# A 64-byte against a 192-byte offset for one half of the stationary weights' split buffers, in a two-block transformer kernel on one core

## The chip, the cores and the metric

The kernel runs on one core of one Trainium2 chip. The metric is the device time of one execution in microseconds: the median of three runs. Lower is better.

## The reference, cut to what matters

Two transformer blocks run one after the other over 256 tokens of width 1024, in float32. They hold six feed-forward stages, an mLSTM and gating mixer, a pooling and SSD mixer, and an attention mixer. Most of the work is products of the tokens with large weights:

```
def swiglu(x, w_in, w_out):
    gate, up = jnp.split(x @ w_in, 2, axis=-1)
    return (jax.nn.silu(gate) * up) @ w_out

x = x + 0.5 * swiglu(rmsnorm(x, ffn1_norm_g[l]), ffn1_w_in[l], ffn1_w_out[l])
proj = xn @ w_mix_in[l]
```

## The kernel before, in words

**Splitting.** Each float32 factor `a` is written as a rounded part `hi` (type fp32r) and a remainder `lo = a - hi`, and a product is three matmuls, `ah*bh + ah*bl + al*bh` (`mm3`, lines 508 to 512). The normalised and transposed tokens stand in `xh` and `xl`, each `[128, 8, 256]`: eight slices of 128 channels with 256 tokens.

**Weights.** They come from memory in units. SyncE's queue loads raw tiles (`_load_raw`), and `_split_one` (line 337) splits one unit: ScalarE writes `hi` (line 357), VectorE writes `lo` (line 358). The two halves stand in one buffer `t` of shape `[128, 2, DP]`, with `DP = D + 64 = 1088` elements of 4 bytes: 1024 are used, 64 are spare. There are six such buffers in the pool `split` (tile name `sp`), and up to eight slots that stages lend while they don't need them (tile name `sx`).

**Two ways to use a unit.** In token mode (`in_chunk`, `out_pass`, `out_half_pass`) the tokens are stationary and the weights stream past, 512 columns a matmul, in the attention stage also 384 and 288. In channel mode the weights are stationary and the tokens stream, 256 columns a matmul. A channel-mode unit is a `cols` unit whose sixth field is 8 (`_mtile`): 128 output channels, with all eight slices of 128 by 128 side by side. `chan_chunk` (in `ffn`, from its third chunk on, output tile `tp`) and `m_tile` (in `mix` and `ssd`, output tile `mm`) take such a unit and make 24 matmuls of it, for each slice `k` one on line 510 (`hi`, streaming `xh`), one on line 511 (`hi`, streaming `xl`) and one on line 512 (`lo`, streaming `xh`). Every matmul has a weight load of its own (PEld in the profile), which TensorE runs while the matmul before it still streams.

```
o = SHIFT if self.units[u][0] == "cols" and self.units[u][5] == 8 else 0
hi, lo = t[:, 0, o:o + D], t[:, 1, o:o + D]
```

**Where the bytes stand.** For a channel-mode unit both parts begin `SHIFT = 16` elements, 64 bytes, into their half; for all other units at 0. The pools put every split buffer, every slot, and `xh` and `xl` 192 bytes past a multiple of 512 bytes in each partition (from the allocated addresses: the first split buffer at 40640, `xh` at 161472, `xl` at 169664). A half is 4352 bytes, 256 past a multiple of 512. So, counted modulo 512, a slice of `hi` of a channel-mode unit begins at 192 + 64 = 256, a slice of `lo` at 192 + 256 + 64 = 0, and the tokens that stream past begin at 192.

**Order.** The program's order on each engine is fixed when it is built (`tick`, `pump`, `after`): splits run ahead of use as buffers come free.

Of the kernel before, what the change touches and what calls it, by code (L numbers as in the profile page):

```python
# [14 lines left out]
D = 1024  # L15
# [7 lines left out]
NEG = -1.0e30  # L23


DP = D + 64
SHIFT = 16

# [88 lines left out]
def _size(u):  # L119
    return D if u[0] == "rows" else u[5] * sum(b - a for a, b in u[3])  # L120
# [112 lines left out]
class Builder:  # L233
# [103 lines left out]
    def _split_one(self):  # L337
        u = self.next_split
        gi, base, last = self.group_of[u]
        while self.next_raw <= gi:  # L340
            self._load_raw()
        n = _size(self.units[u])
        src = self.raws[gi][:, base:base + n]
        if self.main_free:
            self.main_free -= 1
            self.where[u] = None
            t = self.p_split.tile([P, 2, DP], F32R, tag="sp", name="sp")
        else:
            w = self.extra_free.pop(0)
            self.where[u] = w  # L350
            t = self.slot(w, [P, 2, DP], F32R, "sx") if w < 8 else None
        if t is None:
            hi, lo = (self.p_gate.tile([P, D], F32R, tag="gate", name="sg") for _ in range(2))
        else:
            o = SHIFT if self.units[u][0] == "cols" and self.units[u][5] == 8 else 0
            hi, lo = t[:, 0, o:o + D], t[:, 1, o:o + D]
        self.nc.scalar.activation(out=hi[:, 0:n], in_=src, func=AF.Copy)  # L357
        self.nc.vector.tensor_tensor(out=lo[:, 0:n], in0=src, in1=hi[:, 0:n], op=ALU.subtract)  # L358
        self.ready[u] = (hi, lo)
        self.next_split += 1  # L360
        if last:
            del self.raws[gi]
            while self.next_raw < len(self.offs) and len(self.raws) < self.RAW_BUFS:
                self._load_raw()
# [1505 lines left out]
```

## Time and profile before

| | |
|---|---|
| median of 3 runs | 1651.04 us (1649.2 to 1651.7) |
| the profiled execution's own time | 1650.13 us |
| its span, first to last instruction | 1648.3 us |
| around the span | 1.8 us |
| granted TensorE clock, mean | 0.996 of full speed |
| TensorE matmul (PE) busy | 1612.2 us, 98% |
| TensorE weight load (PEld) busy | 1446.2 us, 88% |
| VectorE / ScalarE / GpSimd busy | 1180.0 / 821.1 / 53.2 us |
| moved from memory | 361 MB, 220 GB/s over the span |

Matmuls overlap in the pipeline, so the busy time of one matmul (276 to 281 ns in channel mode) is not what it costs. What it costs is its *step*: the time from its start to the start of the next one. The timeline view shows starts, and a step is read from a long stretch as the last start less the first, over the number of matmuls between.

### The profile page before, as it was taken

Reading aid. Unit: us, or ns where it says so; the run is one execution under the profiler, and the core shown is the slowest. Engines: PE = TensorE matmul, PEld = TensorE weight load, DVE = VectorE, ACT = ScalarE, POOL = GpSimd, SP = SyncE. Lnnn points to the kernel's source line nnn. Section 1 sums busy time; section 2 is a strip of 40 time slices with the busy share of each in tenths; the row PEclk is TensorE's granted clock in tenths of the full one; section 3 lists DMA queues with packets and bytes.
Section 4 is the critical chain, followed back from the end, with each engine's and each line's share of the span. In section 5 each row is a group of like instructions: output and inputs, shape, how many; then the busy total and the mean of one; then the engine's idle time right before and its main releaser. Section 6 shows DMA issues by size and latency. Waiting matters only on the chain.

```text
span 1648.3 us, 25287 instructions
## 1 busy us (share of the span) xinstructions
PE 1612.2 (98%) x10290; PEld 1446.2 (88%) x10290; DVE 1180.0 (72%) x1729; ACT 821.1 (50%) x1161; POOL 53.2 (3%) x81
## 2 busy tenths in 40 slices
PE   8999999999999999999999999999999999999997
PEld 6999889888799988999898789998999987879996
DVE  6699578796688866877687777766777576676653
ACT  6544465445554446444465464445444366555442
POOL 0000001100000000000004000000000010000000
PEclk9999999999999999999999999999999999999999
DMA  8789344666488845888244269873788343147640
GB/s 296 278 320 329 143 178 154 233 252 225 189 308 292 288 161 206 319 302 297 101 156 152 102 252 340 296 287 119 285 299 296 140 170 151 52 179 256 226 170 26
DMA packets 62469, 363.80 MB, mean 221 GB/s; under 512 B 7056, under 2 KB 7184, under 8 KB 28944
## 3 DMA queue, kind: packets, MB, share of 16 engines
q1 hardware_dynamic: 62208, 362.10, 60.8%
q8 instruction: 81, 1.33, 0.3%
q14 instruction: 36, 0.29, 0.1%
q10 hardware_dynamic: 144, 0.08, 0.0%
HBM read 361.11 MB, written 1.05 MB: 220 GB/s over the span
## 4 chain that ended last, share of the span: by engine, by line
PE 90%; DVE 4%; ACT 4%; issue 1%; DMA 1%; POOL 0%; POOLq 0%; SPq 0%; ACTq 0%; DVEq 0%
PE tp L512 14%; PE tp L510 14%; PE tp L511 14%; PE mm L510 7%; PE mm L512 7%; PE mm L511 7%; PE mm L695 7%; PE mm L696 7%; PE mm L702 7%; DVE sp L358 1%; ACT sp L357 1%; PE tp L623 1%; DMA raw<-in_wts 1%; ACT xn L640 1%; ACT xn L591 1%
## 5 line engine op out<-in xcount | busy, mean ns | idle before, releaser
L358 DVE TENSOR_TENSOR sp<-raw,sp 128x1024 fp32r<-128x1024 f32 (+2 forms) x375 | 453.6, 1220 | 214.7 <-ACT sp L357 213.7
L357 ACT ACTIVATE sp<-raw 128x1024 fp32r<-128x1024 f32 (+2 forms) x375 | 390.0, 1050 | 378.9 <-PE tp L512 202.8
L510 PE MATMUL tp<-xh,sp 128*128 128x256 f32 x1032 | 289.7, 281 | 0.2 <-ACT gate L468 0.2
L512 PE MATMUL tp<-xh,sp 128*128 128x256 f32 x1032 | 289.1, 280 | 0.0
L511 PE MATMUL tp<-xl,sp 128*128 128x256 f32 x1032 | 289.1, 280 | 0.0
L358 DVE TENSOR_TENSOR sx<-raw,sx 128x1024 fp32r<-128x1024 f32 x161 | 196.2, 1221 | 92.3 <-ACT sx L357 92.0
L357 ACT ACTIVATE sx<-raw 128x1024 fp32r<-128x1024 f32 x161 | 169.4, 1055 | 172.5 <-PE tp L512 121.6
L511 PEld LDWEIGHTS tp<-xl,sp 128*128 128x128 f32 x1032 | 197.3, 191 | 0.9
L510 PE MATMUL tp<-xh,sx 128*128 128x256 f32 x696 | 195.8, 281 | 0.8 <-ACT gate L468 0.8
L512 PE MATMUL tp<-xh,sx 128*128 128x256 f32 x696 | 195.4, 281 | 0.0
L511 PE MATMUL tp<-xl,sx 128*128 128x256 f32 x696 | 195.4, 281 | 0.0
L510 PEld LDWEIGHTS tp<-xh,sp 128*128 128x128 f32 x1032 | 193.7, 188 | 1.4 <-ACT gate L468 0.5
L512 PEld LDWEIGHTS tp<-xh,sp 128*128 128x128 f32 x1032 | 193.8, 188 | 0.0
L432 DVE SCALAR_TENSOR_TENSOR mraw<-mraw,c_act 128x1024 f32<-128x1024 f32 x144 | 175.3, 1218 | 0.0
L510 PE MATMUL mm<-sp,xh 128*128 128x512 f32 (+2 forms) x340 | 133.0, 391 | 1.8 <-ACT xh L644 1.8
L511 PEld LDWEIGHTS tp<-xl,sx 128*128 128x128 f32 x696 | 133.3, 192 | 0.9
L510 PEld LDWEIGHTS tp<-xh,sx 128*128 128x128 f32 x696 | 130.6, 188 | 1.9 <-ACT gate L468 1.0
L512 PEld LDWEIGHTS tp<-xh,sx 128*128 128x128 f32 x696 | 130.7, 188 | 0.0
L512 PE MATMUL mm<-sp,xl 128*128 128x512 f32 (+2 forms) x340 | 130.0, 382 | 0.2
L511 PE MATMUL mm<-sp,xh 128*128 128x512 f32 (+2 forms) x340 | 129.4, 381 | 0.0
L695 PE MATMUL mm<-sp,hT 128*128 128x512 f32 x246 | 96.6, 393 | 1.8 <-ACT hT L869 1.4
L696 PE MATMUL mm<-sp,hT 128*128 128x512 f32 x246 | 96.2, 391 | 0.0
(472 smaller groups left out, 2793.3 us busy)
## 6 DMA issues: line engine op xcount, KB each, us to landing
raw<-in_wts SPq DMA_DIRECT2D x260, 1024.0 KB, 5.3
mraw<-in_mod SPq DMA_DIRECT2D x144, 512.0 KB, 5.5
raw<-in_wts SPq DMA_DIRECT2D x4, 768.0 KB, 4.6
raw<-in_wts SPq DMA_DIRECT2D x5, 512.0 KB, 5.2
row<-in_rows SPq DMA_DIRECT2D x3, 512.0 KB, 5.9
raw<-in_wts SPq DMA_DIRECT2D x2, 576.0 KB, 4.0
rows<-in_rows SPq DMA_DIRECT2D x2, 512.0 KB, 6.5
bp<-in_pool SPq DMA_DIRECT2D x1, 1024.0 KB, 7.6
```

What stands on the lines that cost most here:

```text
L357: self.nc.scalar.activation(out=hi[:, 0:n], in_=src, func=AF.Copy)
L358: self.nc.vector.tensor_tensor(out=lo[:, 0:n], in0=src, in1=hi[:, 0:n], op=ALU.subtract)
L432: nc.vector.scalar_tensor_tensor(out=src, in0=src, scalar=1.0, in1=self.c_act, op0=ALU.mult, op1=ALU.mult, accum_out=acc[:, kt:kt + 1])
L510: nc.tensor.matmul(out, ah, bh, start=first, stop=False)
L511: nc.tensor.matmul(out, ah, bl, start=False, stop=False)
L512: nc.tensor.matmul(out, al, bh, start=False, stop=last)
L591: nc.scalar.activation(out=xn[:, sl], in_=x[:, sl], func=AF.Square, scale=1.0 / 32.0, accum_out=ss[:, h:h + 1])
L623: nc.tensor.transpose(ps[:, j, :], src[:, k * P:(k + 1) * P], self.ident)
L640: nc.scalar.activation(out=vb[1][:, j], in_=banks[1][:, j], func=AF.Identity, scale=g[:, 4 + j:5 + j], bias=sh[:, 4 + j:5 + j])
L695: nc.tensor.matmul(accs[t][h], ah, hi[:, sl], start=(k == 0), stop=False)
L696: nc.tensor.matmul(accs[t][h], ah, lo[:, sl], start=False, stop=False)
L702: nc.tensor.matmul(accs[t][h], al, hi[:, sl], start=False, stop=False)
```

## The change

The offset becomes a pair: `hi` stays 16 elements (64 bytes) into its half, `lo` stands 48 elements (192 bytes) into its half. This holds for channel-mode units only.

```
-SHIFT = 16
+SHIFT = (16, 48)
...
-            o = SHIFT if self.units[u][0] == "cols" and self.units[u][5] == 8 else 0
-            hi, lo = t[:, 0, o:o + D], t[:, 1, o:o + D]
+            a, b = SHIFT if self.units[u][0] == "cols" and self.units[u][5] == 8 else (0, 0)
+            hi, lo = t[:, 0, a:a + D], t[:, 1, b:b + D]
```

No instruction is added, removed or moved: on all five engines the two programs have the same instructions in the same order with the same waits, and every tile has the same address. What differs is one address in 244 splits (the output of line 358, once for each channel-mode unit) and in 1952 matmuls and their loads (line 512 with a stationary `lo`, eight for each unit). Modulo 512, the `lo` slices move from 0 to 128; `hi` stays at 256, the streaming tokens at 192. The remainder then ends at element 48 + 1024 = 1072 of 1088.

## Rows read from the trace of the kernel before

**Rows 1.** The page: busy time by engine, and the chain that ended last.
```profile
PE 1612.2 (98%) x10290; PEld 1446.2 (88%) x10290; DVE 1180.0 (72%) x1729; ACT 821.1 (50%) x1161; POOL 53.2 (3%) x81
...
PE 90%; DVE 4%; ACT 4%; issue 1%; DMA 1%; POOL 0%; POOLq 0%; SPq 0%; ACTq 0%; DVEq 0%
```

**Rows 2.** Groups by line and form, PE: operands, count | busy us, mean ns | idle before.
```profile
L510 PE MATMUL tp<-xh,sp 128*128 128x256 f32 x1032 | 289.7, 281 | 0.2 <-ACT gate L468 0.2
...
L510 PE MATMUL tp<-xh,sx 128*128 128x256 f32 x696 | 195.8, 281 | 0.8 <-ACT gate L468 0.8
...
L510 PE MATMUL mm<-xh,sp 128*128 128x256 f32 x224 | 63.8, 285 | 0.0
```

**Rows 3.** Timeline of PE, a whole chunk (start, duration, instruction): one slow stretch.
```profile
59.63 0.28 PE L510 MATMUL tp<-xh,sp 128*128 128x256 f32 x1
...
70.94 0.40 PE L695 MATMUL mm<-sx,hT 128*128 128x512 f32 x1
```

**Rows 4.** Timeline of PE, three units of a later chunk: one fast stretch.
```profile
176.26 0.28 PE L510 MATMUL tp<-xh,sp 128*128 128x256 f32 x1
...
184.42 0.40 PE L695 MATMUL mm<-sp,hT 128*128 128x512 f32 x1
```

**Rows 5.** Groups of weight loads by form, stretch 59.8 to 70 us (slow).
```profile
L511 PEld LDWEIGHTS tp<-xl,sp 128*128 128x128 f32 x16 | 3.1, 192 | 0.0
L512 PEld LDWEIGHTS tp<-xh,sp 128*128 128x128 f32 x16 | 3.0, 188 | 0.0
L510 PEld LDWEIGHTS tp<-xh,sp 128*128 128x128 f32 x15 | 2.8, 188 | 0.0
```

**Rows 6.** The same, stretch 174 to 184 us (fast).
```profile
L512 PEld LDWEIGHTS tp<-xh,sp 128*128 128x128 f32 x23 | 4.3, 188 | 0.0
L511 PEld LDWEIGHTS tp<-xl,sp 128*128 128x128 f32 x23 | 4.3, 188 | 0.0
```

**Rows 7.** Groups of weight loads by form, whole span.
```profile
L511 PEld LDWEIGHTS tp<-xl,sp 128*128 128x128 f32 x1032 | 197.3, 191 | 0.9
L512 PEld LDWEIGHTS tp<-xh,sp 128*128 128x128 f32 x1032 | 193.8, 188 | 0.0
...
L511 PEld LDWEIGHTS tp<-xl,sx 128*128 128x128 f32 x696 | 133.3, 192 | 0.9
L512 PEld LDWEIGHTS tp<-xh,sx 128*128 128x128 f32 x696 | 130.7, 188 | 0.0
...
L511 PEld LDWEIGHTS mm<-xl,sp 128*128 128x128 f32 x224 | 42.2, 188 | 0.1
L512 PEld LDWEIGHTS mm<-xh,sp 128*128 128x128 f32 x224 | 42.1, 188 | 0.0
```

**Rows 8.** Timeline of PE, stationary weights of 8 columns (tile skw), 256 streamed.
```profile
214.88 0.28 PE L510 MATMUL tp<-xh,skw 128*8 128x256 f32 x1
...
216.75 0.28 PE L511 MATMUL tp<-xl,skw 128*8 128x256 f32 x1
216.86 0.28 PE L512 MATMUL tp<-xh,skw 128*8 128x256 f32 x1
...
217.54 0.28 PE L512 MATMUL tp<-xh,skw 128*8 128x256 f32 x1
```

**Rows 9.** Timeline of PE, token mode with 384 and with 288 streamed columns.
```profile
1338.05 0.33 PE L512 MATMUL mm<-sp,xl 128*128 128x384 f32 x1
...
1340.65 0.33 PE L512 MATMUL mm<-sp,xl 128*128 128x384 f32 x1
...
1346.35 0.29 PE L512 MATMUL mm<-sp,xl 128*128 128x288 f32 x1
...
1347.95 0.29 PE L512 MATMUL mm<-sp,xl 128*128 128x288 f32 x1
```

**Rows 10.** Groups by form: the splits on VectorE, and what VectorE waited for.
```profile
L358 DVE TENSOR_TENSOR sp<-raw,sp 128x1024 fp32r<-128x1024 f32 x364 | 444.0, 1230 | 205.9 <-ACT sp L357 204.9
...
L358 DVE TENSOR_TENSOR sx<-raw,sx 128x1024 fp32r<-128x1024 f32 x160 | 195.2, 1223 | 91.1 <-ACT sx L357 90.8
```

## The prediction

> **What bounds the kernel now.** Read the page first: TensorE's matmuls cover 98% of the span and 90% of the chain that ended last [rows 1]. Then the groups by form, for the matmuls whose weights the change touches: 1032 + 696 + 224 on line 510, and as many on lines 511 and 512, so 3 × 1952 = 5856 channel-mode matmuls. They hardly ever wait: 0.2, 0.8 and 0.0 us of idle time on line 510 [rows 2]. So what counts is the step from one start to the next, and a nanosecond on each step is 5.9 us of the kernel.
>
> Then the timeline, and there the steps fall into two paces. In the chunk from 59.63 to 70.94 us, 96 matmuls take 11.31 us: 117.8 ns a step [rows 3]. From 176.26 to 184.42 us, 72 matmuls of the same form take 8.16 us: 113.3 ns a step [rows 4]. Same operands' shapes, same clock, same addresses modulo 512; the streams fall into one pace or the other and then hold it for microseconds. I call them slow and fast; they are 4.5 ns apart.
>
> The weight loads show where the slow pace differs. In the slow stretch one load in three takes 192 ns, the others 188 [rows 5]; in the fast stretch all take 188 [rows 6]. This gives the count of slow steps. Over the span, the loads of line 511 are longer than those of line 512 by 197.3 - 193.8 = 3.5 us, 133.3 - 130.7 = 2.6 us and 0.1 us: 6.2 us in all [rows 7]. At 4 ns each that is 1550 slow trios of 1952, so 4650 slow steps and 1206 fast ones. It is an estimate: in `mix` and `ssd` the long load need not be on line 511, so slow steps may be missing.
>
> **The change part by part.**
>
> *Instructions.* None is added, removed or moved on any engine or queue, no wait is added, and no DMA changes. Nothing to price.
>
> *The write of the remainder.* VectorE's 244 outputs on line 358 land 128 bytes further on. The splits of the two buffer kinds, which mix shifted and unshifted outputs, take 1230 and 1223 ns [rows 10]; if the place cost or gave those 7 ns it would be 244 × 7 = 1.7 us of VectorE work, under the 205.9 + 91.1 us that VectorE idles ahead of these very instructions [rows 10]. The cover is that TensorE does not wait for splits [rows 2]; without it the 1.7 us would show. I take 0.
>
> *The read of the remainder.* This is the whole question: 1952 loads read from another place while `xl` streams, and nothing in the trace shows a stationary operand at 128 modulo 512 in channel mode. So the price is bounded from both sides by the nearest rows.
>
> - Gain, near end: only the stretch of the long load goes. That is 6.2 us if all of it was on the path [rows 7]. A second row agrees in size: with stationary weights of 8 columns, where hardly anything is loaded, 16 steps of the slower pace take 216.75 - 214.88 = 1.87 us, 116.9 ns a step [rows 8], 0.9 ns under 117.8; on 4650 steps that is 4.2 us.
> - Gain, in proportion: one load in three is moved, and the steps that it decides go at the fast pace: 1550 × 4.5 ns = 7.0 us [rows 3, 4].
> - Gain, far end: the slow pace can't keep itself up once one of its three loads is changed, and all slow steps become fast: 4650 × 4.5 ns = 20.9 us. That a slow stretch can fall into the fast pace and stay is seen in the 8-column weights: from 216.86 to 217.54 us, six steps take 0.68 us, 113.3 ns [rows 8].
> - Loss: token mode shows a still slower step. 15 steps of 384 columns take 2.60 us, 173.3 ns; 12 steps of 288 take 1.60 us, 133.3 ns [rows 9]. The line through them falls by 0.417 ns a column, and at 256 columns it gives 133.3 - 13.3 = 120.0 ns. If all channel-mode steps went to that, it would cost 4650 × 2.2 + 1206 × 6.7 = 10.2 + 8.1 = 18.3 us; if one in three did, 6.1 us.
>
> Between a gain of 20.9 and a loss of 18.3 us I take the gain in proportion, 7.0 us: it is next to the 6.2 us that the load rows carry directly [rows 7], and these are the only rows in which the loads differ between the two paces.
>
> The sum: 1650.1 us for the profiled execution, less 7.0, is 1643.1 us. The median of the runs shown, 1651.0, stands 0.9 us above the profiled execution, so for a median I say 1644.
>
> *A rule that speaks against it.* The rows show the pace of a stream and the length of its loads going together: 192 and 188 ns at 117.8 a step, 188 alone at 113.3 [rows 3 to 6]. The Trainium skill, page "SBUF — State Buffer", section "Who interferes with whom", gives TensorE two independent read ports, one for the streaming operand and one for weight loads, and says that it never waits on anyone. By that rule the place of the remainder changes nothing and the sum would be 1650.1 us. The trace agrees only in part: a port that nobody disturbs does not explain the 4 ns [rows 5, 6].
>
> **The rivals.**
>
> *No change: the place does not matter (1650 us).* The two paces are a matter of phase between loads and streams, not of addresses. For it: `hi` at 256 and `lo` at 0 modulo 512 already stand at different places, and it is a load of `hi` that is long while the load of `lo` is not [rows 5]; the weights of line 510 and line 511 are the very same bytes, and one is long, the other not. The 8-column weights begin at eight places 32 bytes apart, and the pace goes on for 16 steps all the same [rows 8]. Against it: 8-column loads read too little to meet anything for long, and the two places used now differ by 256 bytes, so they say nothing of a difference of 128. Time: 1650.1, between 1647 and 1653.
>
> *The fast stretches are lost (1655.5 us).* The fast pace needs all three steps of a trio at 113.3 ns. If the moved load makes its step just longer than that, no stretch can stay fast: 1206 steps fall back to 117.8, 1206 × 4.5 = 5.4 us more. It decides as soon as the step on line 512 alone exceeds 113.3 ns by any constant amount. For it: the fast pace is the rarer one, 1206 of 5856, and token mode, whose stationary tokens stand level with the streamed weights (192 modulo 512, streams from 192 or 448), never shows it: 133.3 and 173.3 lie on a line to 120.0 [rows 9]. Against it: the loads of `lo` have no long row now [rows 5, 7]. If the slow steps go to 120.0 as well, it is 18.3 us and 1668.4.
>
> *The whole slow pace goes (1629.2 us).* It is the far end of the forecast, not a case of its own: the same mechanism, 20.9 us.
>
> **How the numbers follow.** A difference of 0.2%, 3.3 us, is about what a measurement of this kernel can tell from no change. Forecast, the slow pace is weakened or broken: 0.47. Likeliest within it is 1644, its own range 1628 to 1647. No change: 0.33, because most of what the rows say of addresses is that they don't matter, but none of them tests a step of 128 bytes. Lost fast stretches, or steps towards 120.0: 0.20; there is a row for such a step, and nothing that ties it to this place. Low end: 1650.1 - 20.9 = 1629.2, with a margin 1628. High end: 1657, which takes in no change and the lost fast stretches (1655.5), and leaves out the steps towards 1668. What is left out is about 0.1 above and 0.05 below. So faster 0.47, same 0.33, slower 0.20.
>
> **What would show it.** The forecast is right if the chunk of rows 3 starts its 96 matmuls in clearly less than 11.31 us (11.17 for a third of the steps at the fast pace, 10.88 for all), if the loads of lines 511 and 512 come closer than 6.2 us in sum, and if the splits, the transfers and the token-mode steps stay as they are. It is wrong if the chunk takes 11.31 us again with one 192 ns load in three: then the place does not matter. The rival of lost fast stretches is right if the 72 matmuls of rows 4 take 8.48 us in place of 8.16. The prediction would also be wrong if VectorE's splits changed by more than the 7 ns between their two groups, since then something other than TensorE's reads would be at work.

## The result, and the profile after

| | before | after |
|---|---|---|
| median of 4 runs | 1651.13 us | 1630.45 us (1628.16 to 1632.76) |
| ratio, 95% interval | | 0.9877 [0.9858, 0.9896] |
| the profiled execution's own time / span | 1650.13 / 1648.3 us | 1632.14 / 1630.4 us |
| granted TensorE clock, mean | 0.996 | 0.996 |

The changed kernel is 20.7 us faster by the medians; the interval reaches from 17.2 to 23.4 us. The forecast was 7.0. The profiled execution of the changed kernel is one of its slower ones, so the two profiles are 18.0 us apart; the account below is of these two.

The page of the changed kernel, busy time by engine and the chain that ended last:

```profile
PE 1593.5 (98%) x10290; PEld 1427.6 (88%) x10290; DVE 1179.7 (72%) x1729; ACT 821.8 (50%) x1161; POOL 53.1 (3%) x81
...
PE 89%; DVE 5%; ACT 4%; DMA 1%; issue 1%; POOL 0%; POOLq 0%; SPq 0%; ACTq 0%; DVEq 0%
```

Against [rows 1], the matmuls are busy for 18.7 us less and the loads for 18.6 us less; the other engines differ by less than 1 us. TensorE still sets the time. Now the groups by form of the channel-mode matmuls, lines 511 to 513 (the change adds one line, so `mm3` stands one line further down):

```profile
L511 PE MATMUL tp<-xh,sp 128*128 128x256 f32 x1032 | 285.7, 277 | 0.2 <-ACT gate L469 0.2
...
L511 PE MATMUL tp<-xh,sx 128*128 128x256 f32 x696 | 192.8, 277 | 0.8 <-ACT gate L469 0.8
```

These are the groups of [rows 2], 4.0 and 3.0 us shorter, and each of the three lines has lost about as much. The timeline says how. First the chunk of [rows 3], entered from a token-mode matmul of 512 columns (line 703):

```profile
59.31 0.61 PE L703 MATMUL mm<-sp,hT 128*128 128x512 f32 x2
59.76 0.28 PE L511 MATMUL tp<-xh,sp 128*128 128x256 f32 x1
59.88 0.28 PE L512 MATMUL tp<-xl,sp 128*128 128x256 f32 x1
...
60.47 0.28 PE L511 MATMUL tp<-xh,sp 128*128 128x256 f32 x1
...
60.92 0.28 PE L512 MATMUL tp<-xl,sp 128*128 128x256 f32 x1
...
70.67 0.40 PE L696 MATMUL mm<-sx,hT 128*128 128x512 f32 x1
```

The 96 matmuls take 70.67 - 59.76 = 10.91 us, 113.6 ns a step, where they took 11.31. The stretch starts at the slow pace: its first six steps take 0.71 us, 118 ns each. Then it settles by itself: from 60.92 on, 86 steps take 9.75 us, 113.4 ns. The stretch of [rows 4], which was fast before, comes again to 8.16 us over 72 steps:

```profile
173.59 0.28 PE L511 MATMUL tp<-xh,sp 128*128 128x256 f32 x1
...
181.75 0.40 PE L696 MATMUL mm<-sp,hT 128*128 128x512 f32 x1
```

The long loads are gone. Groups of weight loads by form, whole span, against [rows 7]:

```profile
L512 PEld LDWEIGHTS tp<-xl,sp 128*128 128x128 f32 x1032 | 193.8, 188 | 0.9
...
L513 PEld LDWEIGHTS tp<-xh,sp 128*128 128x128 f32 x1032 | 193.7, 188 | 0.0
...
L513 PEld LDWEIGHTS tp<-xh,sx 128*128 128x128 f32 x696 | 130.7, 188 | 0.0
L512 PEld LDWEIGHTS tp<-xl,sx 128*128 128x128 f32 x696 | 130.7, 188 | 0.9
```

**Unit by unit.** The 5856 channel-mode matmuls are 244 units of 24. I took the mean step of each unit from its 13th matmul on, when it has settled. Before, 46 units had under 115 ns and 198 had 117.8. After, all 244 have 113.3 to 113.6.

**The account of the two profiles.** 198 slow units × 24 × 4.5 ns = 21.4 us could go. Summed from the starts in the timeline, the channel-mode steps take 688.3 us before and 668.8 after: 19.5 us less. Of the 1.9 us that are missing, 1.6 lie in the first twelve steps of the units that do not follow another channel-mode unit; these steps stay slow, as in the chunk above. Token mode gives 1.9 us back: the median step of 512 columns is 227 ns in both, but 163 of the 3375 steps are longer than 250 ns, where 154 were, and their sum goes from 804.3 to 806.2 us. 19.5 - 1.9 = 17.6 of the 17.9 us by which the spans differ.

Splits and their slack, groups by form on VectorE:

```profile
L359 DVE TENSOR_TENSOR sp<-raw,sp 128x1024 fp32r<-128x1024 f32 x364 | 444.1, 1230 | 197.5 <-ACT sp L358 196.5
L359 DVE TENSOR_TENSOR sx<-raw,sx 128x1024 fp32r<-128x1024 f32 x160 | 195.2, 1222 | 82.8 <-ACT sx L358 82.4
```

Their durations are those of [rows 10]; VectorE idles 16.7 us less ahead of them: the same work now stands in a shorter kernel.

### The profile page after: what moved, and what is told of

Same layout as the page of the kernel before. It is cut to its first block, busy times and chain, and to the rows that moved or that the text cites. A ratio compares the mean times of both kernels' runs of the same rounds, so it can differ in the third digit from the quotient of the medians.

```text
span 1630.4 us, 25287 instructions
## 1 busy us (share of the span) xinstructions
PE 1593.5 (98%) x10290; PEld 1427.6 (88%) x10290; DVE 1179.7 (72%) x1729; ACT 821.8 (50%) x1161; POOL 53.1 (3%) x81
## 4 chain that ended last, share of the span: by engine, by line
PE 89%; DVE 5%; ACT 4%; DMA 1%; issue 1%; POOL 0%; POOLq 0%; SPq 0%; ACTq 0%; DVEq 0%
PE tp L513 13%; PE tp L511 13%; PE tp L512 13%; PE mm L511 7%; PE mm L513 7%; PE mm L512 7%; PE mm L696 7%; PE mm L697 7%; PE mm L703 7%; DVE sp L359 2%; DMA raw<-in_wts 1%; ACT sp L358 1%; ACT xn L641 1%; PE tp L624 1%; ACT xn L592 1%
## 5 line engine op out<-in xcount | busy, mean ns | idle before, releaser
L511 PE MATMUL tp<-xh,sp 128*128 128x256 f32 x1032 | 285.7, 277 | 0.2 <-ACT gate L469 0.2
L513 PE MATMUL tp<-xh,sp 128*128 128x256 f32 x1032 | 285.1, 276 | 0.0
L512 PE MATMUL tp<-xl,sp 128*128 128x256 f32 x1032 | 285.0, 276 | 0.0
L358 ACT ACTIVATE sx<-raw 128x1024 fp32r<-128x1024 f32 x161 | 169.7, 1057 | 165.1 <-PE tp L513 113.6
L512 PEld LDWEIGHTS tp<-xl,sp 128*128 128x128 f32 x1032 | 193.8, 188 | 0.9
L511 PE MATMUL tp<-xh,sx 128*128 128x256 f32 x696 | 192.8, 277 | 0.8 <-ACT gate L469 0.8
L513 PE MATMUL tp<-xh,sx 128*128 128x256 f32 x696 | 192.3, 276 | 0.0
```

Source lines behind the costliest of these rows:

```text
L511: nc.tensor.matmul(out, ah, bh, start=first, stop=False)
L512: nc.tensor.matmul(out, ah, bl, start=False, stop=False)
L513: nc.tensor.matmul(out, al, bh, start=False, stop=last)
```

## The experiments

All of them move operands by 64 to 384 bytes or add a small matmul; none changes what is computed. To compare places I use the **distance** of a stationary slice: its place less the place of the streaming tokens, modulo 256 bytes. Before, `hi` stands at 256 and `lo` at 0 (modulo 512) and the tokens at 192, so both distances are 64: the pair (64, 64) of (`hi`, `lo`). The change makes it (64, 192). That the places count modulo 256 is itself tested, at one pair (`e5`).

The theories, by the letters that stand for them:

- **P**: only the place of `lo` counts; **D**: only the distance between `hi` and `lo` counts; **S**: the distance of each load to the tokens that stream while it runs counts, for `lo` that is `xl`. That the place does not matter was the prediction's rival.
- **R**: the distances of both parts to the token tiles, modulo 256, decide the pace: slow with both on one side, fast with one on each side. **A**: the places of the parts themselves decide, wherever the tokens stand.
- **E**: the distances decide only which paces can hold themselves; how a run of matmuls is entered chooses among them. **F**: the distances alone decide, and the entry has no part. F has the kernel before against it from the start: there 23 of the 129 units in split buffers (`sp`, output `tp`) and 5 of the 87 in slots (`sx`) have the pace of 113.3 ns, at the same places modulo 512 as the others with 117.8.

"Fast units" below are those of the 244 with a settled step under 115 ns. The ratio is to the kernel before on the same chip.

| run | (`hi`, `lo`) | median, us | ratio, 95% | settled step, ns | fast units |
|---|---|---|---|---|---|
| before | 64, 64 | 1651.1 | 1 | 117.8, 113.3 | 46 |
| after | 64, 192 | 1630.45 | 0.9877 [0.9858, 0.9896] | 113.3 | 244 |
| e1 | 192, 192 | 1654.1 | 1.0032 [1.0021, 1.0043] | 117.8 | 6 |
| e2 | 192, 64 | 1634.0 | 0.9901 [0.9872, 0.9930] | 113.3, 119.0 | 215 |
| e4 | 0, 0 | 1668.5 | 1.0110 [1.0081, 1.0139] | 120.0 | 0 |
| e5 | 64, 64 | 1648.5 | 1.0001 [0.9988, 1.0015] | 117.8, 113.3 | 46 |
| e6 | 64, 128 | 1656.3 | 1.0038 [1.0022, 1.0054] | 118.2 to 118.9 | 0 |
| e11 | 128, 0 | 1657.7 | 1.0050 [1.0036, 1.0064] | 118.2 | 0 |
| e9, tokens moved | 192, 192 | 1657.9 | 1.0048 [1.0030, 1.0066] | 117.8 | 7 |
| e10, tokens moved | 192, 64 | 1661.4 | 1.0067 [1.0041, 1.0093] | 119.0, 113.4 | 18 |
| e3, `xl` moved | mixed | 1656.1 | 1.0034 [1.0023, 1.0045] | 117.5 to 118.2 | 0 |
| e7, after and `xl` moved | mixed | 1672.5 | 1.0140 [1.0119, 1.0160] | 119 to 122 | 0 |

### e1: both parts 192 bytes in

```
-SHIFT = (16, 48)
+SHIFT = (48, 48)
```

> Both parts of a channel-mode unit stand 192 bytes into their half (hi at 384, lo at 128 modulo 512). Theory P (the place of the remainder alone decides): the slow pace is gone, about 1630 us, a trio's loads 188 ns each. Theory D (the distance between the two parts decides, and 256 bytes apart is bad): as before, about 1651 us, one load in three 192 ns. Theory S (each load's distance to the tokens that stream past it decides): hi and lo now both stand where only lo stood in the changed kernel, so no load is at the old distance; about 1630 us.

Measured: 1654.1 us, and 6 fast units in place of 46. **P falls**: `lo` stands where the change puts it, and the gain is gone. S named 1630 us too and misses; D named the time of before. The weight loads of `e1`, groups by form:

```profile
L512 PEld LDWEIGHTS tp<-xl,sp 128*128 128x128 f32 x1032 | 193.9, 188 | 0.9
L513 PEld LDWEIGHTS tp<-xh,sp 128*128 128x128 f32 x1032 | 193.7, 188 | 0.0
L511 PEld LDWEIGHTS tp<-xh,sp 128*128 128x128 f32 x1032 | 193.2, 187 | 1.4 <-ACT gate L469 0.5
```

Nearly every unit runs at 117.8 ns here, and no load is long. So the 192 ns loads of [rows 5] come with the slow pace at (64, 64), but are not what makes it slow.

### e2: the parts changed about, `hi` 192 bytes in and `lo` 64

```
-SHIFT = (16, 48)
+SHIFT = (48, 16)
```

> The rounded part moves instead of the remainder (hi at 384, lo at 0 modulo 512). Theory P: the remainder is where it was, so as before, about 1651 us. Theory D: the two parts are as far apart as in the changed kernel, only the other way round, so about 1630 us. Theory S: the two hi loads of a trio get the new distance and the lo load keeps the old one; two loads in three are cured, so at least part of the gain, 1630 to 1640 us.

Measured: 1634.0 us, nearly all of the gain; 215 units are fast, 29 run at 119.0 ns. Groups by form on PE, line 511:

```profile
L511 PE MATMUL tp<-xh,sp 128*128 128x256 f32 x1032 | 285.8, 277 | 0.2 <-ACT gate L469 0.2
```

It takes 285.8 us, as after (285.7). Two parts 128 bytes apart are better than two at the same distance, whichever of them is moved. P does not foresee it, D does, and S allowed it.

### e3: the kernel before, `xl` begins 384 bytes later

```
-        self.xl = self.p_xT.tile([P, 8, S], F32R, tag="xl", name="xl")
+        xl = self.p_xT.tile([P, 8 * S + 128], F32R, tag="xl", name="xl")
+        self.xl = xl[:, 96:96 + 8 * S].rearrange("p (k s) -> p k s", k=8)
```

> The kernel before, with the weights where they were, and the remainder of the tokens (xl, which streams while lo is loaded) begun 384 bytes later, so that lo stands to it modulo 512 as in the changed kernel. Theory S: about 1630 us, loads 188 ns. Theories P and D: nothing of the weights moved, so as before, about 1651 us with one load in three at 192 ns.

Measured: 1656.1 us, no fast unit. `lo` now stands to `xl` as it does in the changed kernel, and nothing is gained: **S falls**. (The time also holds token-mode matmuls, in which `xl` takes part; the verdict rests on the settled step.)

### e4: no offset at all

```
-SHIFT = (16, 48)
+SHIFT = (0, 0)
```

> No offset at all in channel mode (hi at 192, lo at 448 modulo 512), as the token-mode units have it. Theory D: the parts are 256 bytes apart as before, so about 1651 us. Theory S: hi is level with the streaming tokens; if token mode's line holds for this case, steps of 120.0 ns and about 1668 us. Theory P: lo is at a place not tried yet; anything from 1630 to 1668 us.

Measured: 1668.5 us, each unit at 120.0 ns, and now every load is long (groups by form of `e4`, PE and then PEld):

```profile
L511 PE MATMUL tp<-xh,sp 128*128 128x256 f32 x1032 | 292.5, 283 | 0.2 <-ACT gate L469 0.2
...
L512 PEld LDWEIGHTS tp<-xl,sp 128*128 128x128 f32 x1032 | 198.0, 192 | 0.9
L513 PEld LDWEIGHTS tp<-xh,sp 128*128 128x128 f32 x1032 | 198.0, 192 | 0.0
```

This is the price that the line through the token-mode steps [rows 9] gave for level operands, 120.0 ns and 1668.4 us. It belongs to another place than the change uses. **D misses**: the parts are 256 bytes apart as before, for which it named 1651 us.

### e5: `lo` 192 bytes ahead of its half

```
-            hi, lo = t[:, 0, a:a + D], t[:, 1, b:b + D]
+            flat = t.rearrange("p i n -> p (i n)")
+            hi, lo = flat[:, a:a + D], flat[:, DP + b:DP + b + D]
```

with `SHIFT = (16, -48)`. Modulo 512, `lo` stands 256 bytes from where it stood before; modulo 256 it stands at the same place.

> The remainder is moved the other way, to 256 modulo 512, where the rounded part stands too; 256 bytes from its place before the change, while hi stays. Theory D (the distance of the two parts modulo 256 decides, and 0 is bad): the distance is 0 modulo 512, so as before, about 1651 us, steps near 117.8 ns with one long load in three. Theory P (the place of the remainder decides by itself): 256 is a new place; if only 0 was bad, about 1630 us.

Measured: 1648.5 us, ratio 1.0001; 198 slow and 46 fast units as before, and the long load on the same line (the edits move `mm3` two lines down); groups of weight loads by form of `e5`:

```profile
L513 PEld LDWEIGHTS tp<-xl,sp 128*128 128x128 f32 x1032 | 197.3, 191 | 0.9
L514 PEld LDWEIGHTS tp<-xh,sp 128*128 128x128 f32 x1032 | 193.7, 188 | 0.0
```

These are the values of [rows 7] within 0.1 us. At this pair, what counts is the place modulo 256 bytes.

### e6: `lo` 128 bytes in

As `e5`, with `SHIFT = (16, 32)`.

> The remainder moves half as far as in the change, 128 bytes into its half, so to 64 modulo 512; the parts are 64 bytes apart modulo 256. Theory D, if any distance other than 0 will do: about 1630 us. Theory D, if it must be near 128: between 1630 and 1651 us. Theory P: a new place, either.

Measured: 1656.3 us, no fast unit, 118.2 to 118.9 ns. That is above all that D named for it. The offset of `lo` does not help by being another one than that of `hi`; at 64 bytes more it costs, at 128 more it gives.

### e7: the changed kernel, `xl` begins 384 bytes later

The edit of `e3` on the changed kernel.

> The changed kernel, with the remainder of the tokens moved by 384 bytes, so that every load again stands 64 bytes ahead of the tokens that stream past it, as before the change, while the two parts keep the distance of the changed kernel. Theory D: the distance of the parts is unchanged, so about 1630 us and steps of 113.3 ns. Theory S (a trio must have loads on both sides of its streams): as before, about 1651 us.

Measured: 1672.5 us, no fast unit, steps of 119 to 122 ns, longest in the matmuls that stream `xl` (groups by form of `e7`, PE):

```profile
L512 PE MATMUL tp<-xl,sp 128*128 128x256 f32 x1032 | 295.4, 286 | 0.0
L511 PE MATMUL tp<-xh,sp 128*128 128x256 f32 x1032 | 292.2, 283 | 0.2 <-ACT gate L469 0.2
```

`hi` and `lo` stand 128 bytes apart, as in the changed kernel. **D falls**: the tokens must stand right too. S misses as well: every load stands 64 bytes from the tokens that stream while it runs, as before the change, and it named 1651 us for that.

### e8 and e12: other places for the token-mode units

`e8` gives the changed kernel's pair to all units:

```
-            a, b = SHIFT if self.units[u][0] == "cols" and self.units[u][5] == 8 else (0, 0)
+            a, b = SHIFT
```

> The changed kernel, with the pair of offsets for every unit that stands in a split buffer, so also for those that stream past the tokens in token mode. There the streams then begin at 256 and 128 modulo 512 and the stationary tokens at 192. If the 13.3 ns by which a token-mode step exceeds the line through zero come from operands that stand level, as in channel mode without any offset (120.0 ns, where all stood at 192 modulo 256), the 512-column steps fall from 226.7 to about 220 ns; over 3372 such matmuls 6.7 ns each are 22 us, so about 1608 us. If 13.3 ns are a fixed cost of a matmul of that width, no change: 1630 us.

`e12` leaves channel mode as changed and puts both parts of the other units 128 bytes in: `else (32, 32)` in place of `else (0, 0)`.

> The changed kernel, with the units of token mode begun 128 bytes into their halves. Token-mode steps went from 226.7 to about 230 ns when the pair 64 and 192 was given to those units too, so place counts there as well. If 128 bytes is a better place, steps under 226.7 ns and under 1630 us (each ns is 3.4 us); if level is the best place there, 227 to 230 ns and 1630 to 1640 us.

Measured: 1639.3 us, ratio 0.9943 [0.9926, 0.9959], and 1643.5 us, 0.9961 [0.9946, 0.9975]: both faster than before, both slower than the changed kernel. Neither of the two times named for `e8` came, and `e12` lies above the range for it. Channel mode keeps 244 fast units in both. Token mode loses: the step of 512 columns goes from 227 to 230 and 232 ns. One group of token-mode matmuls on PE, by form, first in the changed kernel:

```profile
L696 PE MATMUL mm<-sp,hT 128*128 128x512 f32 x246 | 96.5, 392 | 2.1 <-ACT hT L870 1.6
```

The same in `e8`:

```profile
L696 PE MATMUL mm<-sp,hT 128*128 128x512 f32 x246 | 98.0, 398 | 1.8 <-ACT hT L870 1.5
```

And in `e12`:

```profile
L696 PE MATMUL mm<-sp,hT 128*128 128x512 f32 x246 | 97.7, 397 | 0.6 <-ACT hT L870 0.5
```

So the 13.3 ns that a token-mode step takes beyond its columns (0.417 ns each, [rows 9]) do not come from level operands alone; two other places cost more.

### e9 and e10: both token tiles moved, 384 bytes

`e9` is the kernel before and `e10` the changed kernel, each with

```
+        xh = self.p_xT.tile([P, 8 * S + 128], F32R, tag="xh", name="xh")
+        xl = self.p_xT.tile([P, 8 * S + 128], F32R, tag="xl", name="xl")
+        self.xh, self.xl = (v[:, 96:96 + 8 * S].rearrange("p (k s) -> p k s", k=8) for v in (xh, xl))
```

The weights stay where they were. Counted from the tokens, `e9` has the distances of `e1`, and `e10` those of `e2`.

> The kernel before, with both token tiles (xh and xl) begun 384 bytes later, so at 64 modulo 512, and the weights left alone. Theory R (only the distances of the loads to the streaming tokens count, modulo 256; both parts on the same side give the slow pace, one part on each side the fast one): both parts stand 192 ahead modulo 256, as where both parts had been moved; about 1654 us, and 117.8 ns in nearly all units, hardly any at 113.3. Theory A (the places of the parts themselves count): as before, 1650 us, 46 of 244 units under 115 ns. The stationary tokens of token mode move too, which may add a few us: read the channel-mode steps.

> The changed kernel, with both token tiles begun 384 bytes later. Theory R: the parts stand 192 and 64 ahead of the tokens modulo 256, mirrored against the changed kernel, as where the rounded part alone had been moved; so the fast pace in most units and some 20 units near 118.8 ns, about 1634 us. Theory A: the places are those of the changed kernel, 113.3 ns in nearly all units and 1630 us. If moving the remainder of the tokens alone was bad because the rounded part and the remainder of the tokens then stood at different places, this run must not show the 120 to 122 ns of that one.

Measured: `e9` 1657.9 us, 117.8 ns and 7 fast units, the picture of `e1` (117.8 and 6) from the other side. Its span is 3.8 us over that of `e1`, and its token-mode steps of 512 columns sum to 808.3 us against 804.5: those with `xh` or `xl` as the stationary operand, which stands elsewhere too, take 232 ns, the others 227 as in `e1`. Its channel-mode steps sum to 692.1 us, as in `e1`. That agrees with R, and A, which named 46 fast units, falls. `e10` has the two paces of `e2`, 113.4 and 119.0 ns, but in the other proportion: 18 fast units, where `e2` has 215. The groups by form of `e10`, PE:

```profile
L512 PE MATMUL tp<-xl,sp 128*128 128x256 f32 x1032 | 291.4, 282 | 0.0
L511 PE MATMUL tp<-xh,sp 128*128 128x256 f32 x1032 | 288.4, 279 | 0.2 <-ACT gate L469 0.2
```

So the distances give the paces that are to be had, and something else picks one. R, which named about 1634 us, is not enough. The two are not alike in all else: modulo 512 `lo` stands 320 bytes from the tokens in `e2` and 64 in `e10`, and `e5` shows only for the pair (64, 64) that such 256 bytes do not count.

### e11: another pair 128 bytes apart

```
-SHIFT = (16, 48)
+SHIFT = (32, 64)
```

> Both parts 64 bytes further on than in the changed kernel: the parts keep their distance of 128 modulo 256, but the rounded part stands 128 from the tokens and the remainder level with them. Theory D (the parts' distance of 128 is enough): about 1630 us, 113.3 ns. Theory R: one load level with its stream, which alone (no offset at all) gave 120.0 ns; so between 1640 and 1668 us.

Measured: 1657.7 us, every unit at 118.2 ns. D misses once more: the parts are 128 bytes apart, in the wrong place relative to the tokens. The time lies within the 1640 to 1668 us that R named.

### e13 to e15: the entry of each unit disturbed

One transpose of 128 columns ahead of each of the 216 units of `chan_chunk`. It is extra work; what it writes is overwritten by the unit's first matmul.

```
                     hi, lo = self.take()
+                    nc.tensor.transpose(o[:, m * S:m * S + P], self.ident, self.ident)
```

`e13` is the kernel before with it, `e14` the changed kernel, `e15` is `e10` with it. Each was run once.

> The kernel before, with one transpose of the identity ahead of each of the 216 units of channel mode in the feed-forward stages, written where the unit's first matmul then writes its product. It breaks the run of matmuls without moving any operand. Theory E (at given addresses more than one pace can hold itself, and how a run is entered chooses): most of these units run at 113.3 ns after the break, as 22 of 27 units did in the kernel before that began after a break; the breaks cost about 0.12 us each, 26 us, and the faster steps give back up to 20 us, so about 1656 us. Theory F (addresses alone set the pace): 117.8 ns as before, and about 1676 us.

> The same breaks in the changed kernel, as the measure of what they cost. Theories E and F: units at 113.3 ns as without them, and 26 us more, about 1656 us. If the break itself makes a run slow, units above 115 ns appear here.

> The same breaks in the changed kernel with both token tiles moved, which ran at 118.8 ns in most units while the same distances modulo 256, made by moving the rounded part, gave 113.3 ns in most. Theory E: the breaks put most units at 113.3 ns, so about 1656 us or below 1660. Theory F: 118.8 ns stays, about 1684 us.

Measured: `e14` has 244 fast units, and its span of 1654.4 us prices the breaks at 24.0 us, 0.111 us each. `e13` takes 1672.4 us in all, span 1670.6: less the breaks, 1646.6, only 1.7 us under the kernel before. By the total, that is near what F leads to. Its units say more. 67 are fast instead of 46, and of the 216 units with a break it depends on what stood ahead of the break: after token mode 32 of 46 go fast, after a channel-mode unit 7 of 158, after a 128-column matmul 10 of 12. Of the 42 breaks right behind a fast channel-mode unit, 36 lead to a slow one. The timeline of PE in `e13`, a first and a second unit:

```profile
110.62 0.39 PE L702 MATMUL mm<-sp,hT 128*128 128x512 f32 x1
110.85 0.27 PE L886 MATMUL tp<-cst 128*128 128x128 f32 x1
110.88 0.37 PE L510 MATMUL tp<-xh,sx 128*128 128x256 f32 x1
...
111.67 0.28 PE L510 MATMUL tp<-xh,sx 128*128 128x256 f32 x1
...
113.71 0.27 PE L886 MATMUL tp<-cst 128*128 128x128 f32 x1
113.74 0.36 PE L510 MATMUL tp<-xh,sp 128*128 128x256 f32 x1
...
114.17 0.28 PE L510 MATMUL tp<-xh,sp 128*128 128x256 f32 x1
...
116.65 0.27 PE L886 MATMUL tp<-cst 128*128 128x128 f32 x1
```

From 111.67 to 113.71 us are 18 steps of 113 ns; after the break, from 114.17 to 116.65 us, 21 steps of 118 ns. Same program, same places modulo 256, two paces, set where the unit begins. The long load has changed its line: in `e13` it is that of `lo`, where in the kernel before it was the second one of `hi` [rows 7], at the same pace (117.7 ns against 117.8). Groups of weight loads by form of `e13`:

```profile
L512 PEld LDWEIGHTS tp<-xh,sp 128*128 128x128 f32 x1032 | 196.8, 191 | 0.0
L511 PEld LDWEIGHTS tp<-xl,sp 128*128 128x128 f32 x1032 | 194.2, 188 | 0.0
```

`e15` has 157 fast units where `e10` has 18, and its span less the breaks is 1668.7 - 24.0 = 1644.7 us, 13.2 under `e10`. So the entry chooses, as E has it; E counted on most breaks leading to the fast pace, with about 1656 us for `e13` and at most 1660 for `e15`, and missed both times (`e15` took 1670.5). F named 1676 and 1684 us and missed too.

The kernel before shows the same by itself. Of its units, 47 begin right behind a 512-column matmul: all 47 are slow. 27 begin behind another matmul that is not of channel mode, most often one of 128 columns, with a first step of over 150 ns: 22 are fast. One follows the 8- or 16-column weights and is slow. The other 169 begin right behind a channel-mode unit, and all 169 run at the pace of the unit ahead, which is why the paces of [rows 3] and [rows 4] hold for whole chunks.

No version beat the changed kernel.

## Why the prediction was right or wrong

**The price of the instructions, and the write of the remainder: right.** VectorE's splits take 1230 and 1222 ns, as before; nothing waits for them that did not before, but for some longer steps in token mode (1.9 us in these two profiles).

**What bounds the kernel: right.** The whole difference lies in the channel-mode step, which has no wait in it, and the two paces of [rows 3] and [rows 4] are what the change works on.

**The step that failed is "Gain, in proportion": 1550 × 4.5 ns = 7.0 us.** It took one load in three as moved and let one step in three go fast. The pace is not a property of one step: all three steps of a trio run at it, the run of matmuls holds it, and a run has one pace or the other. With `lo` moved, no slow pace holds itself at (64, 192): a run that enters at 118 ns leaves it within some six steps. So the settled slow steps all went, and 19.5 us of channel-mode steps with them. That is the far end of the term, 20.9 us, with 1629.2 us as its time, which the prediction priced and put aside; the median is 1630.45.

That the sign came out right was in part luck: by the prediction's own words no row stood at 128 bytes, and with `lo` moved by 64 bytes in place of 128 the same reasoning would have met a loss (`e6`, ratio 1.0038).

**Why the choice between the ends went wrong.** It was made by the row nearest to 7.0: the 6.2 us by which the loads of line 511 are longer [rows 7]. `e1` shows that the slow pace of 117.8 ns exists with all loads at 187 to 188 ns, and `e10` a pace of 119.0 ns with loads of 187 to 188. In `e13` the long load stands on another line at the same slow pace. It went along with the pace at this pair of places and did not carry its cost. It was a good counter all the same: 1550 slow trios estimated, 198 × 8 = 1584 found.

**The evidence for the far end was in the rows.** The 8-column weights of [rows 8] go over into the fast pace and stay there. The prediction cited this and still took a third. What it lacked was the question what begins a pace: that 47 of 47 entries straight from a 512-column matmul are slow, and that 169 of 169 units take over the pace ahead of them, could have been read from the trace of before, and with it that a run carries its pace on from its start.

**No change (0.33): wrong.** The counter-argument, "the two places used now differ by 256 bytes, so they say nothing of a difference of 128", was the right one: `e5` shows that at this pair 256 bytes are no difference at all. The placements take 1630.45 (after) to 1672.5 us (`e7`), with the same instructions. By the rule of the Trainium skill, page "SBUF — State Buffer", section "Who interferes with whom", which gives TensorE two independent read ports and says that it never waits on anyone, all these placements would take 1650 us; the measurement decides: the place matters. That it is a read port that is waited for is not shown.

**The fast stretches are lost, or steps towards 120.0 (0.20): wrong for this change.** The stretch of [rows 4] takes 8.16 us again. The step of 120.0 ns is real, and the line through the token-mode steps had its size exactly, 1668.4 us worked out and 1668.5 measured in `e4`; it belongs to level operands, not to `lo` at 192 bytes. That token mode pays its 13.3 ns for standing level is not borne out: `e8` and `e12` moved its weights and it became slower.

**The signs: right.** 10.91 us for the chunk lies next to 10.88, which was named for all steps fast, far from the 11.17 for a third; the loads of the two lines came closer from 6.2 to 0.1 us; the token-mode steps stayed at 227 ns.

**What stays open.** Why the places count modulo 256 bytes; why at (64, 192) the slow pace can't hold itself and at (64, 64) and (192, 64) both can; what in an entry chooses, beyond the counts above; whether places 256 bytes apart are alike at other pairs than that of `e5`; and what makes up the 6.6 ns by which 113.3 ns exceed 256 columns at the 0.417 ns each of [rows 9]. Offsets in steps finer than 64 bytes were not tried. After a break the pace also goes with the unit's position among the four of a chunk: in `e15` 46 of the 54 first units are fast, 8 of the second, 45 of the third, 52 of the fourth. Each position writes another part of the output tiles, and no run moved that; in the kernel before every unit right behind another runs as that one, whatever its position. So it is shown that a break changes the pace, and not which property of the entry does it.

## What to carry to other kernels

Where a chain of short matmuls, each with its own weight load, is what bounds a kernel, read the steps unit by unit, and if they fall into two paces, price a change by whole runs of units: ask what starts each pace and whether it holds itself, not how many instructions are touched. The place of the stationary operand relative to the streaming one is then worth trying for each part apart, here in steps of 64 bytes over 256, and the effect should be checked from the other side by moving the streaming operand. Such a setting is good for one pair of tiles: the offsets that took 20.7 us off in channel mode made token mode slower.

## What the runs showed that was not expected

- The same 5856 matmuls take 113.3, 117.8, 118.2, 119.0 or 120.0 ns a step depending on where their operands begin within 256 bytes, without a wait that the profile would name: between `e7` and the changed kernel lie 42 us, and the page of each says that TensorE is busy 98% of the span.
- Two paces at one setting, each holding itself over many units, with the choice made at the entry (before: 47 of 47 entries straight from a 512-column matmul slow, 22 of 27 with a long first step fast, 169 of 169 units behind another at its pace). A single added matmul of 0.111 us can switch a unit from one to the other in either direction.
- A weight load that is 4 ns longer is no measure of the cost of its step: it is seen at 117.8 ns (64, 64) and at 120.0 ns (0, 0), and not at 117.8 ns (192, 192); at (64, 64) it changes its line when the entry is disturbed (`e13`), and the step does not.
